# Score passes of the 64-wide heads and the compressed branch's matmuls, all over 128 rows

## The chip, the core and the metric

The program runs on one core of a Trainium2 chip. The metric is the device time of one execution, in microseconds (us). The core has a matrix engine (TensorE, PE in the profile), three engines for elementwise work (VectorE or DVE, ScalarE or ACT, GpSimd or POOL) and SyncE (SP), whose queue issues most of the transfers. TensorE multiplies a stationary operand, loaded beforehand by a weight load (PEld), with a moving one that streams through; the stationary operand has as many rows as the contraction is long. Results go to PSUM.

## The reference, cut to what matters

Two residual blocks over 512 tokens of 1024 features, in float32. Block 1 has latent attention (MLA, 96 wide), a sparse attention (NSA, 8 heads of 64 in 2 groups) and a gated MLP; block 2, twice, has 4 differential heads, 12 heads of 64 and a convolved MLP. The parts at issue are the scores of the 64-wide heads, and the compressed branch of NSA, in which 31 compressed keys and values stand for blocks of 32 tokens:

```
s_c = jnp.einsum('bsgrd,bngd->bgrsn', qg, kc) * scale      # 4 heads r of a group g share 31 keys n
p_c = jax.nn.softmax(jnp.where(valid_c, s_c, NEG), axis=-1) * valid_c
o_c = jnp.einsum('bgrsn,bngd->bsgrd', p_c, vc)
...
s_w = jnp.einsum('bcqgrd,bckgd->bcgrqk', qb, kb) * scale   # window; the selected branch and block 2 alike
```

## The kernel before, in words

**Precision.** Every float32 factor is split into a high and a low part of a shorter format (float32r), `hi` by ScalarE and `lo = x - hi` by DVE, and a product is made of `hi*hi`, `hi*lo` and `lo*hi`, which accumulate in one PSUM tile. A head of 64 has half of the array's rows only, so two of the three parts are stacked: `stack_q` puts the queries' high and low part one above the other into a tile of 128 rows (`qa`, by copies on SP), and the keys' high part lies there twice (`ka`). One pass over 128 rows then gives `qh*kh + ql*kh`. The third part, `qh*kl`, is a second pass over 64 rows (`nqh` with `kl` or `qkl` in the rows of the profile).

**Scores.** `scores` (L904) makes a unit of one head and branch: for each of four blocks of 128 queries both passes, 256, 256, 384 and 512 keys wide (256, 256, 384 and 384 in the window), then the softmax with DVE and ScalarE. All matmuls stand at L103 (`mm`), all transposes at L107 (`tr`). `apply_v` transposes the probabilities, splits them and multiplies with the values into `ps_o`.

**Compressed branch.** `cmp_end` makes the compressed keys and values: `kcA` (high part, twice) and `kcL` (low part, twice) with 32 columns for each group, and `vcA`, high and low beside each other, with the same 32 rows four times, for the four heads. `cmp_scores` makes for each head a tile of 32 rows of scores, which ScalarE copies (L1333) into the head's rows of `sT`; and the unit of the window ends with two passes over the 32 rows of its head:

```
mm(ps[:32], kcA[:, g], qa, True, False)
mm(ps[:32], kcL[ro:ro + 64, g], qhi, False, True)
...
mm(po, vcA[rr, g], pch[rr], False, False)
mm(po, vcA[rr, g], pcl[rr], False, True)
```

**Order.** Generators weave the attention units (`pipeline`: the preparation of a unit, the scores of the one before, the values of the one before that) with a filler, the projections and output products whose matmuls write `ps_d` (`merge`). Behind that a scheduler lays out the instructions of each engine before the run, by its own model of their durations, and decides which tile of a pool goes where; each engine then runs its list in order. Tiles of 128x512 come from one pool, `U`, of 67. SP's list holds the loads of weights (L122, L209, into 4 buffers) and the copies of queries (L1299, L1300) and keys (L1278, L1738).

Of the kernel before, what the change touches and what calls it, by code (L numbers as in the profile page):

```python
# [9 lines left out]
F32R = mybir.dt.float32r  # L10
# [9 lines left out]
NB = S // 128  # L20
# [54 lines left out]
def blocks_kernel(ctx: ExitStack, tc: tile.TileContext, A, out):  # L75
# [72 lines left out]
    def fm_weights(src, nk, c0, ncols, r0=0):  # L148
        """Yields (m, [(kt, hi, lo)]) for each tile of 128 columns."""
        for c in range(c0, c0 + ncols, 256):  # L150
            n = min(256, c0 + ncols - c)
            step = 1024 // n
            tiles = [[] for _ in range(n // 128)]
            for k0 in range(0, nk, step):
                k = min(step, nk - k0)
                hi, lo = split(raw_load(src, r0 + 128 * k0, k, c, n))
                for i in range(k):
                    for q in range(n // 128):
                        cs = slice(128 * q, 128 * q + 128)
                        tiles[q].append((k0 + i, hi[:, i, cs], lo[:, i, cs]))  # L160
            for q in range(n // 128):
                yield (c - c0) // 128 + q, tiles[q]

    def fm_start(parts, nk, X):
        """the first two tiles of features of one or two products, k by k; parts: (src, c0, r0, evac)"""
# [18 lines left out]
    def fm_product(src, nk, c0, ncols, X, evac, r0=0, m0=0):  # L184
        """features m0.. of a product whose columns begin at c0"""
# [12 lines left out]
    def tm_product(src, nk, cols, X, evac):  # L198
        """token-major product for the column ranges cols; evac(blk, ps)."""
# [39 lines left out]
    def blend(main, other, ratio):  # L239
        """main's steps, with ratio times as much of other in between; other's cost is not counted"""  # L240
# [22 lines left out]
    def merge(main, filler, ratio, finish=True):  # L263
        """main, with ratio times as much of filler in between. Either may yield a key that the
        other one has to mark before it goes on."""
# [37 lines left out]
    def split_act(src_ap, shape=(128, 512), scale=None, name="x"):  # L303
        """src (fp32) * scale -> hi (ACT), lo (DVE)."""
# [31 lines left out]
    # x, token-major  # L336
# [7 lines left out]
    # per-feature vectors, as columns  # L344
    col = {}

    def load_vectors(eng, name, rows):
# [4 lines left out]
        for nm, ap, n in rows:  # L352
# [3 lines left out]
            elif isinstance(ap, list):  # L356
                # gains that the rotated part of a head does not take here
# [15 lines left out]
    # masks  # L373
# [20 lines left out]
    def rsqrt_cols(dst, src, n):  # L394
        """dst = (src / n + eps) ** -0.5 on small tiles."""
# [10 lines left out]
    # silu(c)  # L406
# [11 lines left out]
    def ada_sums(ws, pool=False, n=512):  # L418
        """per-partition part of a modulation group; ws: list of the group's 8 weight tiles, which
        receives the sum"""  # L420
# [23 lines left out]
    def ada(g):  # L444
        """columns 512g.. of the modulation"""
# [17 lines left out]
    def adas(groups):  # L463
        """the modulation's column groups; each one's sum over partitions follows later"""
# [10 lines left out]
    # the first product, for six tiles of features at once, by quarters of its rows: each quarter  # L475
    # needs its own columns of the first shift and scale only
# [3 lines left out]
    # (first tile of rows, tiles)  # L480
# [27 lines left out]
    # small loads, for later  # L508
# [92 lines left out]
    def mod1_end(c):  # L601
        """a chunk's features of the first shift and scale"""
# [13 lines left out]
    def mod1_step(q, n):  # L616
        """the next n (all with 0) of a quarter's sums"""
# [8 lines left out]
    def angles():  # L626
        """positions times frequencies, and a quarter turn more, in -pi..pi"""
# [154 lines left out]
    def gain_tables(name, tab, gains, half):  # L782
        """tables for a rotation after the gains; one set for each head"""
# [17 lines left out]
    def rope(eng, v, tab, b, half, n, p=128):  # L801
        """v: [p, n, >=2*half]; rotates the first 2*half of the last dim in place."""
# [16 lines left out]
    # compressed blocks: key n ends at 16 n + 31  # L819
# [8 lines left out]
    # lambda of the differential heads  # L828
# [32 lines left out]
    def vsplit(dst, src, scale=None):  # L861
        """dst [128, n, 128] <- src [128, n, 64]: hi | lo"""
# [31 lines left out]
    def to_fm(src, w, o=0):  # L894
        """src: list of NB token-major [128, >=o+w]; -> psum [w, 512]"""
# [8 lines left out]
    def scores(passes, mask, scale, kind, res, gate=None, tok=None):  # L904
        """res gets (P, r): softmax numerators P[q] [128, n] and (gate over denominators) r [128, 4].
        scale is a power of two, so that the scaled scores are exact; tok: a positive factor of each
        query's scores, and its negative."""
# [53 lines left out]
    def apply_v(P, kind, po, vf, start, stop):  # L961
        """transposes P, splits it and accumulates the product with V in po"""
# [32 lines left out]
    def pipeline(units, WO, LAG):  # L995
        """units: generator functions (prep, first, second, perhaps third), each stage one unit
        behind the one before it"""
# [10 lines left out]
    def weave(*gens):  # L1008
        """alternates the steps of generators, each taking its number of steps"""
# [10 lines left out]
    def o_pair(pair, po, i, res, name):  # L1020
        """sums the two halves of po into rows 64i.. of the pair's tile"""
# [134 lines left out]
    # compressed keys and values  # L1156
    CT = [[], []]

    def cmp_prep(i):
        """keys (0) or values (1) and positions, arranged for the product with w1"""  # L1160
# [28 lines left out]
    def cmp_hidden(i):  # L1189
# [12 lines left out]
        # silu through tanh, times two  # L1202
# [10 lines left out]
    kcA = cp.tile([128, 2, 32], F32R, name="kcA")  # L1213
    kcL = cp.tile([128, 2, 32], F32R, name="kcL")
    vcA = cp.tile([128, 2, 128], F32R, name="vcA")
    V.memset(f32(kcA), 0.0)
    V.memset(f32(kcL), 0.0)

    def cmp_end():
        w2k, w2v = (load_w2(A[n][0]) for n in ("cmp_w2_k", "cmp_w2_v"))  # L1220
# [33 lines left out]
        vsplit(vcA, pvc)  # L1254
# [9 lines left out]
        SC.copy(kcA[:, :, 0:31], pk3)  # L1264
        V.tensor_tensor(kcL[:, :, 0:31], pk3, f32(kcA[:, :, 0:31]), op=OP.subtract)
        yield 1.0

    # keys: [hi; hi] and [lo; lo] for both groups
    def dup_keys(o):
        kh, kl = split_act(to_fm([flat(t) for t in NK], 128, o), scale=vcol(("nsa_ks", "nsa_kw")[o // 128], 0),  # L1270
                           name="nk")
        res = []
        for g in range(2):
            own = slice(64 * g, 64 * g + 64)
            a = U(dt=F32R, name="ka")
            l = U(dt=F32R, name="kl")
            for i in range(2):
                nc.sync.dma_start(out=f32(a[64 * i:64 * i + 64]), in_=f32(kh[own]))  # L1278
                nc.sync.dma_start(out=f32(l[64 * i:64 * i + 64]), in_=f32(kl[own]))
            res.append((a, l))  # L1280
        return res
# [9 lines left out]
    def stack_q(src, o, scale=None):  # L1291
        """two heads of 64: H [128,512] and for each head the stacked parts"""
# [9 lines left out]
        return qh, ql, st  # L1302
# [10 lines left out]
    def nsa_units(g):  # L1313
# [3 lines left out]
        def stacks():  # L1317
            yield from need("nsa")
            for pr in range(2):
                qh, ql, st = stack_q([flat(t) for t in NQ], 256 * g + 128 * pr, vcol("nsa_q", 0))  # L1320
                yield 0.43
                for i in range(2):
                    heads.append((st[i], qh[64 * i:64 * i + 64], 64 * i))

        def cmp_scores():
            # compressed branch, four heads at once
            yield from need("cmp")
            sT = U(name="sT")
            for r_, (qa, qhi, ro) in enumerate(heads):
                ps = PS("s", bufs=3)  # L1330
                mm(ps[:32], kcA[:, g], qa, True, False)
                mm(ps[:32], kcL[ro:ro + 64, g], qhi, False, True)
                SC.copy(sT[32 * r_:32 * r_ + 32], ps[:32])  # L1333
                yield 0.43
            ps = PS("t")
# [28 lines left out]
        def unit(r_, br, hd):  # L1364
# [4 lines left out]
            def first():  # L1369
                rate[0] = RU[4 * g + r_]  # L1370
                qa, qhi, ro = heads[r_]
                ka, kl = (KS_, KW_)[br - 1][g]
                st["P"] = []
                yield from scores([(qa, ka), (qhi, kl[ro:ro + 64])], (maskC, maskW)[br - 1], SC8, kind,
# [3 lines left out]
            def second():  # L1378
# [5 lines left out]
                if br == 2:  # L1384
                    pch, pcl = sm["pc"]
                    rr = slice(32 * r_, 32 * r_ + 32)
                    mm(po, vcA[rr, g], pch[rr], False, False)
                    mm(po, vcA[rr, g], pcl[rr], False, True)
# [13 lines left out]
    # merge gates, y = (1 + tanh(z / 2)) * (o @ w_o)  # L1402
# [27 lines left out]
    # residual, feature-major  # L1430
# [31 lines left out]
    def sq_acc(acc, m, src):  # L1462
        """squares of the features; the last tile's stay apart"""
# [7 lines left out]
    def rstd_tm(acc, r):  # L1471
        """r [128, 4] <- (mean of squares + eps) ** -0.5 of the tokens"""
# [9 lines left out]
    def rstd_fm(acc, res):  # L1482
        """the same over the free dimension, for all partitions; in PSUM"""
# [7 lines left out]
    def beside(main, side, at):  # L1491
        """takes a step of side after each of the steps at of main"""
# [36 lines left out]
    def dilated_mask():  # L1529
# [4 lines left out]
        # multiplicity of a distance in the three dilated patterns, as 8*log(m)  # L1534
# [20 lines left out]
    def alternate(a, b, n):  # L1555
        """n steps of a, n of b, ..."""
# [47 lines left out]
    for l in range(2):  # L1604
# [15 lines left out]
        # quads of heads: (columns of q, k, v), group size, rope table, half, mask, first pair of outputs  # L1620
# [101 lines left out]
        def head_unit(P_, h, pair, mask, o0, tag, ratio):  # L1722
            st = {}
            pr, hh = divmod(h, 2)
            own = slice(64 * hh, 64 * hh + 64)

            def prep():
                yield from need(tag)
                if hh == 0:
# [4 lines left out]
                    kas = []  # L1734
                    for j in range(2):
                        ka = U(dt=F32R, name="ka")
                        for i in range(2):
                            nc.sync.dma_start(out=f32(ka[64 * i:64 * i + 64]), in_=f32(kh[64 * j:64 * j + 64]))  # L1738
                        kas.append(ka)
# [184 lines left out]
```

## Time and profile before

| | |
|---|---|
| Time, median of 3 runs | 2229.66 us (2229.32 to 2234.01) |
| Profiled execution, span | 2226.2 us |
| PE busy | 2157.5 us, 97% |
| DVE busy | 1373.3 us, 62% |
| ACT busy | 977.3 us, 44% |
| POOL busy | 311.1 us, 14% |
| DMA queue of SP | 226.01 MB, 33.8% of 16 engines |

The span goes from the first to the last instruction of one profiled execution; the times of the runs hold what lies around it as well, and the page gives no other time for the profiled execution. The attention of block 1 with its filler ends at about 480 us; block 2's attention takes 978 to about 1205 us in the first layer and 1612 to about 1840 us in the second. In a row, `128*128 128x512` is the stationary operand's rows and columns and then the moving operand's. The end of a matmul is modelled, and matmuls are pipelined, so that two of them overlap in the rows; the distance from start to start is what one takes of the engine.

### The profile page before, as it was taken

To read this page: it belongs to the slowest core of one execution; us is meant where nothing else is said; L and a number is where in the kernel's file an instruction comes from. 1 tells how busy PE (TensorE), PEld (TensorE's weight loads), DVE (VectorE), ACT (ScalarE), POOL (GpSimd) and SP (SyncE) were. 2 spreads that over 40 slices of the span, in tenths; PEclk is the share of its full clock that TensorE was granted. 3 is DMA by queue.
4 is the path that set the end of the run, shared out by engine and by line. 5 is a ranking of instruction groups with operands and counts; after the bars stand their busy time and mean duration, and the time that the engine had idled before them with its cause. 6 is when DMAs were issued, how large, how long until landed. Compare 5 with 4: busy or idle time off the path is not lost.

```text
span 2226.2 us, 28323 instructions
## 1 busy us (share of the span) xinstructions
PE 2157.5 (97%) x10349; PEld 1760.7 (79%) x10349; DVE 1373.3 (62%) x2557; ACT 977.3 (44%) x1756; POOL 311.1 (14%) x409
## 2 busy tenths in 40 slices
PE   5999899999999999999999999999999999999998
PEld 4878677777788888888877888888878877888887
DVE  6657877658554333536878673665357787754662
ACT  4456554452322232335655442343356655432441
POOL 4332400003100000111101110011111102100111
PEclk9999999999999999999999999999999999999999
DMA  8222443225343232333333233323344322323231
GB/s 258 80 73 67 116 121 101 80 86 206 98 148 107 85 114 90 98 106 87 96 103 87 87 109 97 104 77 103 95 115 110 90 76 85 114 89 110 77 110 60
DMA packets 211491, 229.09 MB, mean 103 GB/s; under 512 B 12590, under 2 KB 182234, under 8 KB 211352
## 3 DMA queue, kind: packets, MB, share of 16 engines
q1 hardware_dynamic: 209592, 226.01, 33.8%
q8 instruction: 82, 1.34, 0.3%
q0 software_dynamic: 640, 0.55, 0.2%
q10 hardware_dynamic: 1120, 0.72, 0.1%
q14 instruction: 57, 0.47, 0.1%
HBM read 202.06 MB, written 2.10 MB: 92 GB/s over the span
## 4 chain that ended last, share of the span: by engine, by line
PE 71%; DVE 2%; ACT 0%; issue 0%; DMA 0%; DVEq 0%; ACTq 0%
PE ps_d L103 62%; PE ps_s L103 4%; PE ps_t L107 3%; PE ps_o L103 2%; PE ps_t L103 0%; DVE wlo L143 0%; DVE X L1779 0%; ACT p L935 0%; DVE hl L312 0%; DVE p L1707 0%; DMA gf<-in_g_final 0%; DVE p L959 0%; ACT qk L1638 0%; DVE p L931 0%; DVE outt L1895 0%
## 5 line engine op out<-in xcount | busy, mean ns | idle before, releaser
L143 DVE TENSOR_TENSOR wlo<-raw,whi 128x1024 fp32r<-128x1024 f32 (+3 forms) x338 | 415.7, 1232 | 199.6 <-ACT whi L142 196.5
L142 ACT CAST whi<-raw 128x1024 fp32r<-128x1024 f32 (+3 forms) x344 | 346.3, 1009 | 423.7 <-PE ps_d L103 335.4
L103 PE MATMUL ps_d<-hh,whi 128*128 128x512 f32 x1168 | 466.3, 399 | 9.5 <-ACT hh L665 5.9
L103 PE MATMUL ps_d<-hl,whi 128*128 128x512 f32 x1168 | 459.6, 393 | 3.7 <-DVE hl L666 3.7
L103 PE MATMUL ps_d<-hh,wlo 128*128 128x512 f32 x1168 | 458.3, 392 | 0.0
L103 PEld LDWEIGHTS ps_d<-hh,whi 128*128 128x128 f32 x1168 | 220.7, 189 | 63.0 <-ACT hh L665 7.2
L103 PEld LDWEIGHTS ps_d<-hl,whi 128*128 128x128 f32 x1168 | 221.3, 189 | 48.1 <-DVE hl L666 5.4
L103 PEld LDWEIGHTS ps_d<-hh,wlo 128*128 128x128 f32 x1168 | 220.8, 189 | 45.7 <-issue 0.2
L103 PE MATMUL ps_d<-whi,hh 128*128 128x512 f32 (+3 forms) x608 | 219.6, 361 | 1.7 <-DVE v L869 1.0
L103 PE MATMUL ps_d<-whi,hl 128*128 128x512 f32 (+3 forms) x608 | 210.9, 347 | 0.0
L103 PE MATMUL ps_d<-wlo,hh 128*128 128x512 f32 (+3 forms) x608 | 210.1, 346 | 0.0
L103 PE MATMUL ps_d<-fl,whi 128*128 128x512 f32 x528 | 205.6, 389 | 0.0
L103 PE MATMUL ps_d<-fh,whi 128*128 128x512 f32 x528 | 205.6, 389 | 0.0
L103 PE MATMUL ps_d<-fh,wlo 128*128 128x512 f32 x528 | 205.6, 389 | 0.0
L935 ACT ACTIVATE p<-p,sm 128x384 f32<-128x384 f32 (+3 forms) x256 | 144.5, 566 | 69.9 <-DVE sm L931 59.5
L1835 DVE SCALAR_TENSOR_TENSOR ca<-cu,cvT,ca 128x511 f32<-128x511 f32 (+1 forms) x176 | 132.5, 758 | 32.3 <-ACT ca L1833 30.6
L1469 POOL TENSOR_TENSOR acc<-acc,sq 128x512 f32<-128x512 f32 x36 | 56.8, 1578 | 603.3 <-ACT sq L1467 602.6
L1857 POOL TENSOR_TENSOR ca<-ca 128x512 f32<-128x512 f32 x44 | 61.9, 1407 | 520.8 <-DVE ca L1835 472.9
L103 PEld LDWEIGHTS ps_d<-whi,hh 128*128 128x128 f32 x608 | 115.7, 190 | 16.7 <-issue 4.3
L103 PEld LDWEIGHTS ps_d<-whi,hl 128*128 128x128 f32 x608 | 115.5, 190 | 11.9 <-issue 0.5
L103 PEld LDWEIGHTS ps_d<-wlo,hh 128*128 128x128 f32 x608 | 115.8, 191 | 8.0
L1833 ACT ACTIVATE ca<-cu,cvT 128x512 f32<-128x512 f32 x88 | 71.5, 815 | 108.4 <-DVE cu L1831 107.4
(479 smaller groups left out, 3531.9 us busy)
## 6 DMA issues: line engine op xcount, KB each, us to landing
raw<-in_w_up SPq DMA_DIRECT2D x88, 512.0 KB
raw<-in_w_in SPq DMA_DIRECT2D x60, 512.0 KB
aw<-in_ada_w SPq DMA_DIRECT2D x88, 256.0 KB
raw<-in_w_down SPq DMA_DIRECT2D x32, 512.0 KB
raw<-in_ffn_w_gate SPq DMA_DIRECT2D x22, 512.0 KB
raw<-in_ffn_w_up SPq DMA_DIRECT2D x22, 512.0 KB
raw<-in_w_out SPq DMA_DIRECT2D x16, 512.0 KB
raw<-in_ffn_w_down SPq DMA_DIRECT2D x16, 512.0 KB
```

The costliest lines, as they stand in the source:

```text
L103: PE.matmul(o, lhsT=l, rhs=r, start=start, stop=stop)
L107: PE.transpose(o, i, ident[:n, :n])
L142: a = SC.copy(hi, raw)
L143: b = eng.tensor_tensor(lo, raw, f32(hi), op=OP.subtract)
L935: SC.activation(P[q], P[q], AF.Exp, scale=-1.0 if tok is None else tok[1][:, q:q + 1], bias=mn[:, q:q + 1], accum_out=den[:, q:q + 1])
L1469: G.tensor_tensor(acc[0], acc[0], t, op=OP.add)
L1833: SC.activation(a, u, AF.Identity, scale=cvT[:, l, 2, j:j + 1], bias=cvT[:, l, 3, j:j + 1])
L1835: V.scalar_tensor_tensor(a[:, i:], u[:, :S - i], cvT[:, l, 2 - i, j:j + 1], a[:, i:], op0=OP.mult, op1=OP.add)
L1857: G.tensor_tensor(a, a, SG[m], op=OP.mult)
```

## The change

Second passes of scores take the whole of `qa` instead of the high part of the queries, and the keys' low part is laid out twice (`kl`, by copies, also in block 2, where it was used in place). The pass then adds `ql*kl` as well, a fourth part that was left out before. The compressed keys of a group lie in columns 96 to 126 of a tile of zeros, 224 wide; a window of 128 columns is taken from it so that the head's scores fall into rows 32r to 32r+31, and all four heads accumulate into one PSUM tile, which is copied once. The compressed values of a group lie in four tiles of 128 rows, zero but for the head's 32 rows.

```
+    kcA, vcA = [], []
+    def cmp_tiles():
+        for _ in range(2):
+            kcA.append(U((128, 2, 224), F32R, "kcA"))
+            vcA.append(U((128, 4, 128), F32R, "vcA"))
+        for t in kcA + vcA:
+            G.memset(f32(t), 0.0)
...
-        vsplit(vcA, pvc)
+        for r_ in range(4):
+            rr = slice(32 * r_, 32 * r_ + 32)
+            for g in range(2):
+                vsplit(vcA[g][rr, r_:r_ + 1], pvc[rr, g:g + 1])
...
+        for g in range(2):
+            SC.copy(kcA[g][:, 0, 96:127], pk3[:, g])
+            V.tensor_tensor(kcA[g][:, 1, 96:127], pk3[:, g], f32(kcA[g][:, 0, 96:127]), op=OP.subtract)
...
+    def twice(kh, kl, o):
+        res = []
+        for src, name in ((kh, "ka"), (kl, "kl")):
+            t = U(dt=F32R, name=name)
+            for i in range(2):
+                nc.sync.dma_start(out=f32(t[64 * i:64 * i + 64]), in_=f32(src[o:o + 64]))
+            res.append(t)
+        return res
...
+            ps = PS("s", bufs=3)
+            for r_, qa in enumerate(heads):
+                win = slice(96 - 32 * r_, 224 - 32 * r_)
+                mm(ps, kcA[g][:, 0, win], qa, r_ == 0, False)
+                mm(ps, kcA[g][:, 1, win], qa, False, r_ == 3)
                 yield 0.43
+            SC.copy(sT, ps)
...
-                yield from scores([(qa, ka), (qhi, kl[ro:ro + 64])], (maskC, maskW)[br - 1], SC8, kind,
+                yield from scores([(qa, ka), (qa, kl)], (maskC, maskW)[br - 1], SC8, kind,
...
-                    mm(po, vcA[rr, g], pch[rr], False, False)
-                    mm(po, vcA[rr, g], pcl[rr], False, True)
+                    mm(po, vcA[g][:, r_], pch, False, False)
+                    mm(po, vcA[g][:, r_], pcl, False, True)
...
-                    pair["k"] = (kas, kl)
+                    pair["k"] = [twice(kh, kl, 64 * j) for j in range(2)]
...
-                yield from scores([(stk[hh], kas[hh]), (qh[own], kl[own])], mask, SC8, "full", st["P"])
+                yield from scores([(stk, ka), (stk, kl)], mask, SC8, "full", st["P"])
```

The scheduler's lists change with it. In block 1 they stay as they were but for the operands and a few places around the compressed branch; in block 2 the scores and their filler are laid out anew. Three places follow.

TensorE, block 2, the first score unit of a layer, before (`ka` and `qkl` are the keys' parts, `qa` and `nqh` the queries', `ps_d` the filler):

```order
L103 MATMUL ps_s<-ka,qa 128x256
L103 MATMUL ps_s<-qkl,nqh 128x256
L103 MATMUL ps_s<-ka,qa 128x256
L103 MATMUL ps_s<-qkl,nqh 128x256
L103 MATMUL ps_s<-ka,qa 128x384
L103 MATMUL ps_s<-qkl,nqh 128x384
L103 MATMUL ps_s<-ka,qa 128x512
L103 MATMUL ps_s<-qkl,nqh 128x512
```

The same place now:

```order
L103 MATMUL ps_s<-ka,qa 128x256
L103 MATMUL ps_s<-ka,qa 128x384
L103 MATMUL ps_s<-ka,qa 128x512
L103 MATMUL ps_d<-whi,hl 128x512
L103 MATMUL ps_d<-whi,hh 128x512
L103 MATMUL ps_d<-wlo,hh 128x512
L103 MATMUL ps_d<-whi,hl 128x512
L103 MATMUL ps_s<-kl,qa 128x256
L103 MATMUL ps_s<-ka,qa 128x256
L103 MATMUL ps_s<-kl,qa 128x256
L103 MATMUL ps_s<-kl,qa 128x384
L103 MATMUL ps_s<-kl,qa 128x512
```

The first three `ka` passes now come first, then four matmuls of the filler, then the `kl` passes.

SyncE, block 2, the copies of the first pair of 64-wide heads, before:

```order
L1299 DMA qa<-nqh 64x512
L1300 DMA qa<-nql 64x512
L1299 DMA qa<-nqh 64x512
L1300 DMA qa<-nql 64x512
L1738 DMA ka<-qkh 64x512 x4
L209 DMA raw<-in_w_in 128x2x512
```

The same place now:

```order
L1309 DMA qa<-nqh 64x512
L1310 DMA qa<-nql 64x512
L1309 DMA qa<-nqh 64x512
L1310 DMA qa<-nql 64x512
L1284 DMA ka<-qkh 64x512 x2
L1284 DMA kl<-qkl 64x512 x2
L1284 DMA ka<-qkh 64x512 x2
L1284 DMA kl<-qkl 64x512 x2
L209 DMA raw<-in_w_in 128x2x512
```

Each pair has four more copies of 64x512, ahead of the next load of weights.

TensorE, block 1, where the compressed scores stand between the last transposes and value products of MLA (`p`, `mv`); the list of before with -, of now with +:

```order
+L103 MATMUL ps_s<-qa,kcA 128x512 x2
 L107 MATMUL ps_t<-ident,p 128x128 x4
-L103 MATMUL ps_s<-qa,kcA 32x512
-L103 MATMUL ps_s<-nqh,kcL 32x512
+L103 MATMUL ps_s<-qa,kcA 128x512
 L107 MATMUL ps_t<-ident,p 128x128 x2
-L103 MATMUL ps_s<-qa,kcA 32x512
-L103 MATMUL ps_s<-nqh,kcL 32x512
-L103 MATMUL ps_o<-pth,mv 128x512
+L103 MATMUL ps_s<-qa,kcA 128x512
```

The passes keep their number; the first two now stand ahead of the transposes, and the value product that stood between them has moved forward.

## Rows read from the trace of the kernel before

**Rows 1.** Stretch, length; PE, PEld, DVE, ACT, POOL busy us; clock; DMA share; GB/s.

```profile
310.00:480.00 170.00, 169.57 (x782) 121.89 (x781) 118.86 (x363) 85.21 (x212) 0.00 (x0) 0.99 0.22 66
978.00:1050.00 72.00, 72.00 (x391) 58.07 (x390) 42.63 (x112) 40.16 (x93) 10.61 (x24) 1.00 0.40 109
1050.00:1090.00 40.00, 38.78 (x245) 33.91 (x244) 34.40 (x91) 25.10 (x60) 4.31 (x9) 1.00 0.43 117
1090.00:1205.00 115.00, 115.00 (x611) 90.42 (x609) 91.59 (x233) 65.39 (x156) 9.31 (x20) 1.00 0.30 85
```

**Rows 2.** TensorE in order of time: start us, us, engine, line, operation, output<-inputs.

```profile
306.33 0.39 PE L103 MATMUL ps_o<-ptl,mv 128*128 128x512 f32 x1
306.56 0.40 PE L103 MATMUL ps_s<-qa,kcA 128*32 128x512 f32 x1
306.88 0.42 PE L103 MATMUL ps_s<-nqh,kcL 64*32 64x512 f32 x1
307.23 0.44 PE L103 MATMUL ps_o<-pth,mv 128*128 128x384 f32 x1
307.51 0.33 PE L103 MATMUL ps_o<-ptl,mv 128*128 128x384 f32 x1
307.68 0.40 PE L103 MATMUL ps_s<-qa,kcA 128*32 128x512 f32 x1
...
1130.41 0.28 PE L103 MATMUL ps_d<-whi,hl 128*128 128x256 f32 x1
1130.53 0.28 PE L103 MATMUL ps_d<-whi,hh 128*128 128x256 f32 x1
```

**Rows 3.** TensorE in order of time: one score unit of block 2.

```profile
987.48 0.28 PE L103 MATMUL ps_s<-ka,qa 128*128 128x256 f32 x1
987.69 0.38 PE L103 MATMUL ps_s<-qkl,nqh 64*128 64x256 f32 x1
988.00 0.38 PE L103 MATMUL ps_s<-ka,qa 128*128 128x256 f32 x1
...
989.80 0.50 PE L103 MATMUL ps_s<-qkl,nqh 64*128 64x512 f32 x1
990.23 0.50 PE L103 MATMUL ps_d<-whi,hl 128*128 128x512 f32 x1
990.57 0.28 PE L103 MATMUL ps_s<-ka,qa 128*128 128x256 f32 x1
```

**Rows 4.** TensorE and its weight loads in order of time.

```profile
1121.38 0.18 PEld L103 LDWEIGHTS ps_s<-qkl,nqh 64*128 64x128 f32 x1 [0.24 <-issue]
1121.38 0.49 PE L103 MATMUL ps_s<-qkl,nqh 64*128 64x512 f32 x1
```

**Rows 5.** Groups by form, TensorE: busy us, mean ns, idle before.

```profile
L103 PE MATMUL ps_s<-kl,qh 96*128 96x256 f32 x16 | 4.7, 295 | 0.0
L103 PE MATMUL ps_s<-qkl,nqh 64*128 64x256 f32 x48 | 18.3, 381 | 0.0
```

**Rows 6.** TensorE in order of time: compressed values of a head.

```profile
339.64 0.50 PE L103 MATMUL ps_o<-pch,vcA 32*128 32x512 f32 x1
339.99 0.39 PE L103 MATMUL ps_o<-pcl,vcA 32*128 32x512 f32 x1
340.31 0.38 PE L103 MATMUL ps_s<-ka,qa 128*128 128x256 f32 x1
```

**Rows 7.** SyncE in order of time: key copies of a pair.

```profile
983.50 2.45 SPq L1738 DMA_DIRECT2D ka<-qkh  x4
```

**Rows 8.** Waits of the SyncE queue: us in total, times, longest.

```profile
SPq L122 <- DVE wlo L143: 1178.7, 236, 20.4
```

**Rows 9.** Costliest groups of the page: busy us, mean ns, idle before.

```profile
L142 ACT CAST whi<-raw 128x1024 fp32r<-128x1024 f32 (+3 forms) x344 | 346.3, 1009 | 423.7 <-PE ps_d L103 335.4
```

**Rows 10.** All engines in order of time: two small operations.

```profile
299.84 0.29 DVE L866 TENSOR_TENSOR vcA<-ps_t,vcA 128x128 fp32r<-128x128 f32 x1 [0.28 <-ACT vcA L865]
...
1121.75 0.62 POOL L1663 COPY rdx<-sm 128x512 f32<-128x512 f32 x1
```

More of the change, by code (lines that the diff above doesn't have):

```diff
@@ L1211, in load_w2 @@
         return t
[L1213 to L1217, printed above, removed]
+    kcA, vcA = [], []
[5 more added lines that the diff above has]
+            G.memset(f32(t), 0.0)
     def cmp_end():
+        cmp_tiles()
         w2k, w2v = (load_w2(A[n][0]) for n in ("cmp_w2_k", "cmp_w2_v"))
@@ L1263, in cmp_end @@
         pk3 = pkc[:, :62].rearrange("p (g n) -> p g n", g=2)
-        SC.copy(kcA[:, :, 0:31], pk3)
-        V.tensor_tensor(kcL[:, :, 0:31], pk3, f32(kcA[:, :, 0:31]), op=OP.subtract)
+        for g in range(2):
+            SC.copy(kcA[g][:, 0, 96:127], pk3[:, g])
+            V.tensor_tensor(kcA[g][:, 1, 96:127], pk3[:, g], f32(kcA[g][:, 0, 96:127]), op=OP.subtract)
         yield 1.0
+    def twice(kh, kl, o):
[6 more added lines that the diff above has]
+        return res
     def dup_keys(o):
@@ L1271, in dup_keys @@
                            name="nk")
[L1272 to L1281, printed above, removed]
+        return [twice(kh, kl, 64 * g) for g in range(2)]
     SC8 = 0.125
@@ L1301, in stack_q @@
             st.append(t)
-        return qh, ql, st
+        return st
     units = []
@@ L1319, in stacks @@
             for pr in range(2):
-                qh, ql, st = stack_q([flat(t) for t in NQ], 256 * g + 128 * pr, vcol("nsa_q", 0))
+                heads.extend(stack_q([flat(t) for t in NQ], 256 * g + 128 * pr, vcol("nsa_q", 0)))
                 yield 0.43
-                for i in range(2):
-                    heads.append((st[i], qh[64 * i:64 * i + 64], 64 * i))
         def cmp_scores():
@@ L1328, in cmp_scores @@
             sT = U(name="sT")
[L1329 to L1333, printed above, removed]
+            ps = PS("s", bufs=3)
[3 more added lines that the diff above has]
+                mm(ps, kcA[g][:, 1, win], qa, False, r_ == 3)
                 yield 0.43
+            SC.copy(sT, ps)
             ps = PS("t")
@@ L1370, in first @@
                 rate[0] = RU[4 * g + r_]
-                qa, qhi, ro = heads[r_]
+                qa = heads[r_]
                 ka, kl = (KS_, KW_)[br - 1][g]
                 st["P"] = []
-                yield from scores([(qa, ka), (qhi, kl[ro:ro + 64])], (maskC, maskW)[br - 1], SC8, kind,
+                yield from scores([(qa, ka), (qa, kl)], (maskC, maskW)[br - 1], SC8, kind,
                                   st["P"], gv[:, :, h, br])
@@ L1385, in second @@
                     pch, pcl = sm["pc"]
-                    rr = slice(32 * r_, 32 * r_ + 32)
-                    mm(po, vcA[rr, g], pch[rr], False, False)
-                    mm(po, vcA[rr, g], pcl[rr], False, True)
+                    mm(po, vcA[g][:, r_], pch, False, False)
+                    mm(po, vcA[g][:, r_], pcl, False, True)
                     o_pair(hd["pair"], po, h % 2, ON, "on")
@@ L1724, in head_unit @@
             pr, hh = divmod(h, 2)
-            own = slice(64 * hh, 64 * hh + 64)
             def prep():
@@ L1733, in prep @@
                     yield 0.43
[L1734 to L1739, printed above, removed]
-                    pair["k"] = (kas, kl)
+                    pair["k"] = [twice(kh, kl, 64 * j) for j in range(2)]
             def first():
                 rate[0] = ratio
-                qh, _, stk = pair["q"]
-                kas, kl = pair["k"]
+                stk = pair["q"][hh]
+                ka, kl = pair["k"][hh]
                 st["P"] = []
-                yield from scores([(stk[hh], kas[hh]), (qh[own], kl[own])], mask, SC8, "full", st["P"])
+                yield from scores([(stk, ka), (stk, kl)], mask, SC8, "full", st["P"])
                 normalise(*st["P"][0])
```

## The prediction

> **What bounds the kernel now.** I read the stretches first, one row for each stage. In the stages that hold the changed passes, the compressed and selected attention of block 1 (310 to 480 us) and the 64-wide heads of block 2 (978 to 1050 and 1090 to 1205 us; the second layer repeats both from 1612 us), TensorE (PE) is busy for all but 0.43 us of 357, while VectorE (DVE) stands at 70%, 59% and 80% [rows 1]. So these stages end when PE has run its list, and what PE saves there counts, as long as DVE keeps up.
>
> But busy is not the same as streaming. The view in order of time shows this by the distance from one matmul's start to the next one's. In a plain run that distance is 0.12 us for 256 columns, 0.17 for 384 and 0.23 for 512 (the steps from 1130.41, 307.51 and 306.33) [rows 2]. A whole score unit of block 2 looks different [rows 3]: eight passes, alternately 128 rows (`ka,qa`) and 64 rows (`qkl,nqh`), take from 987.48 to 990.23, 2.75 us, where their widths (four of 256, two of 384, two of 512) need 4 x 0.12 + 2 x 0.17 + 2 x 0.23 = 1.28. The full-height matmul behind them still takes 0.34 instead of 0.23. Each step between 128 and 64 rows costs about 0.1 us on either side, and the engine counts as busy meanwhile. The weight loads say why: the load of the 64-row pass starts at 1121.38, in the same 10 ns as its matmul and after 0.24 us of idle that no other engine ended [rows 4]; it isn't loaded beside the matmul before. It is the number of rows and not the second pass as such: MLA's second passes over 96 rows last 295 ns on average at 256 columns, those over 64 rows 381 [rows 5].
>
> **The change part by part.**
>
> *Score passes.* All 160 second passes go from 64 to 128 rows; nothing is added on PE, since a pass takes its columns, and 128-row passes of the same widths keep the plain distance [rows 2]. Per unit that takes away 2.75 - 1.28 + 0.34 - 0.23 = 1.58 us. Units: 8 heads x 2 branches in block 1, and 12 heads x 2 layers in block 2, 40 in all. 40 x 1.58 = 63 us. Units whose passes lie apart between other matmuls cost as much, since each 64-row pass then pays for both its own steps. By stage: 16 units, 25 us, in block 1; 4 units, 6 us, in 978 to 1050; 8 units, 13 us, in 1090 to 1205; the last two again in the second layer.
>
> *Compressed scores.* Per head now 128x32 and 64x32: from 306.56 to 307.23 and 0.28 for the 384-wide matmul behind, against 0.23 + 0.23 + 0.17 [rows 2]: 0.32 us, 8 heads, 2.6 us. The new form has the same two passes, over 128 rows and all 128 columns.
>
> *Compressed values.* Two 32-row passes per head: 0.35 and 0.32 instead of 0.23 each [rows 6], and about 0.1 before and behind as above: 0.40 x 8 = 3.2 us. The rows of zeros cost nothing on PE.
>
> The row of 306.33 shows that going from 128x128 to 128x32 costs nothing: 0.23 to the next start [rows 2]. The Trainium skill (TensorEngine Tiling, Key Properties) says that a change of tiling mode, which there includes tiling by columns, drains the engine; by that the step into the 32 columns should cost another 0.1, 8 times, and the sum would be 0.8 us more. The row decides: only the step in rows is counted.
>
> Gross: 63 + 2.6 + 3.2 = 69 us.
>
> *DVE behind a faster PE.* If the stages shrank by this much, 310 to 480 (all the compressed work and 16 units, 31 us) would last 139 us with 118.86 us of DVE, 86%; 1090 to 1205 would last 102 with 91.59, 90%; 978 to 1050, 66 with 42.63, 65% [rows 1]. The nearest row is the stage of differential heads, 1050 to 1090, where DVE stands at 86% and PE is without work for 1.22 us of 40, 3% [rows 1]. I take 3% of 139 and 4% of 102 twice: 4 + 8 = 12 us given back. The ends: nothing, if all of DVE's idle time is slack; and 31 + 2 x 13 = 57 us, if DVE's idle time in these stages (51 and 23 us) doesn't shrink at all because it is the latency of softmax steps that PE waits for in its fixed order.
>
> *Keys through a transfer.* Block 2 gets four more copies of 64x512 per pair of heads, 12 pairs, 48 in all. Four of them occupy SP for 2.45 us [rows 7]. Queued behind them on SP are the weight loads. Those wait for the release of their buffers anyway (SP's wait on the low parts of weights, 1178.7 us in total) [rows 8], and ScalarE's idle before it splits weights is ended mostly by PE (335.4 of 423.7 us) and not by a transfer [rows 9]: I take nothing, and 12 x 2.45 = 29 us is the far end. The waiting instruction on PE is now the `kl` pass, with all of PE's list behind it. In the first pair of a layer the first key copy is issued at 983.50 and its first pass starts at 987.48, 4 us later [rows 3, 7]; `kl` follows two issues (1.2 us) behind, so it may be ready up to 1.2 us later than `ka`. The new order puts two more `ka` passes and four others (0.17 + 5 x 0.23, about 1.3 us) in between, which covers it: nothing taken, 2 x 1.2 = 2.4 us at the far end; later pairs are prepared a whole unit ahead. Below nothing I see no reason for either.
>
> *Compressed branch, small work.* Seven more splits of 32 rows on ScalarE and on DVE, each as long as the nearest row, 0.29 us, at most: 2 us on each, in 280 to 310; one more split of keys. Four clears of 448 or 512 columns on GpSimd, by its copy of 512 columns 0.62 us each, 2.5 us [rows 10], at the start of the last step of the compressed keys. ScalarE copies the scores once per group instead of four times, off the path. I take 1 us lost; the ends are 0 and 4.5. The four tiles now lie in the common pool until block 1's attention ends, and the high parts of the queries are freed earlier in exchange (four tiles when both groups are up): nothing.
>
> Sum: -69 + 12 + 0 + 1 = -56 us on a profiled span of 2226.2, so 2170. The profile gives its own execution as this span only; the timed runs' median is 3.5 us above it (2229.66), for what lies around, and I keep that: 2174 us.
>
> **The rivals.**
>
> (a) Softmax latency takes over: PE reaches the transposes of a unit before DVE has normalised them, and most of the gain in the dense stages turns into waits. For it: 90% of DVE in 1090 to 1205. Against: PE waits for almost nothing there today, and some of DVE's idle 51 and 23 us must be slack [rows 1]. With half of the 57 us lost instead of 12: -69 + 28 + 1, 2190; with all of it, 2219. It decides from about 30 us of waits on.
>
> (b) The 64-row passes don't pay for their height but for something they keep, say the switch of key tile in the same bank, and the change does nothing to them: then only small losses, 2229 to 2233. Against: the 96-row passes, which have the same switch and last 295 ns [rows 5].
>
> (c) The passes lose an overlap. Two halves of the array could work beside each other, and a 128-row pass would take that away. The place is the step from a 64-row pass into its neighbours; the price, if each of the 160 passes had been half hidden, is half a pass, 0.08 us on average (80 passes of 256 columns, 48 of 384, 32 of 512): 13 us on top, and no gain, 2243. The Trainium skill (TensorE: Matmul & The Clock Gate, Part 3: Packing small matmuls) has the rule: passes of few rows at different row positions run concurrently, so that padding them to 128 gives speed away. Here it decides only if any 64-row pass starts early, and none does: the distance around it grows, to 0.31 at 256 columns [rows 3], which speaks against this case.
>
> (d) PE gains more than I take, because DVE costs it nothing: 2226.2 - 68 + 3.5, 2162.
>
> **How the numbers follow.** My forecast, 2165 to 2190 with 2174 as the value: 0.72. (d), 2157 to 2165: 0.12. (a) beyond 2190: 0.11. (b): 0.03. (c) or a larger loss through the new transfers: 0.02. About 4.5 us, 0.2%, is what a measurement here can tell from no change. All cases but (b) and (c) are faster: 0.95, with 0.03 for the same and 0.02 for slower. For 8 in 10 I take 2158 to 2193.
>
> **What would show it.** Right: starts of `kl,qa` passes 0.12, 0.17 or 0.23 us behind the `ka` pass, loads of weights lying beside the matmul before, PE's share about as high as now over a shorter span, DVE's share up to 84 to 90% in the dense stages, with 10 to 15 us of new waits of PE on DVE or ScalarE. Wrong: the distance around `kl,qa` stays at 0.31 (b), or PE's idle before transposes and value products adds up to more than 30 us (a), or PE waits at the first `kl` pass of pairs for its copy.

## The result and the profile after

The changed kernel takes 2180.29 us (median of 4 runs, 2176.72 to 2182.13) against 2231.34 for the kernel before: a ratio of 0.9773, 95% interval [0.976, 0.9786], 51 us faster. The prediction said 2174, with 2158 to 2193 for 8 in 10.

The profiled spans are 2226.2 and 2180.2, 46 us apart. Of the 5 us between that and the timed gain, 3.2 lie between the first matmul and the first MLA score, where TensorE (PE) has the same list in both: 136.65 us in the trace of before, 139.82 in the trace of after, with a granted clock of 0.91 and 0.86 between 60 and 100 us of the latter. Over all profiles below this stretch comes out at 136 to 140 us, whatever the kernel, so I leave it out of the comparison.

The stages follow from the starts of the same matmuls in both traces, in us. A quad is four heads of block 2: A the differential ones, B, C and D the 64-wide ones; the last row is called the tail below.

| stage | before | changed | difference | gross gain predicted |
|---|---|---|---|---|
| first compressed score to block 1's output product | 182.5 | 153.5 | -29.0 | 31 |
| block 2, quad C, per layer | 55.5 | 49.6 | -5.9, -5.9 | 6 |
| block 2, quad A (unchanged passes) | 57.7 | 57.7 | 0 | 0 |
| block 2, quads B and D (first B to last D score) | 91.5 | 86.3, 85.8 | -5.2, -5.8 | 13 |
| from there to the sums of the next norm | 35.6 | 36.9 | +1.3, +1.2 | 0 |

So the gain is there almost whole in block 1 and in quad C, and some 8.5 us per layer are missing from quads B and D and the tail behind them.

What the change was to do on PE, it did. Two stretches in order of time from the trace of after, which answer to [rows 3] and [rows 6]:

```profile
962.93 0.39 PE L103 MATMUL ps_d<-whi,hl 128*128 128x512 f32 x1
963.15 0.28 PE L103 MATMUL ps_s<-kl,qa 128*128 128x256 f32 x1
963.27 0.28 PE L103 MATMUL ps_s<-ka,qa 128*128 128x256 f32 x1
963.39 0.46 PE L103 MATMUL ps_s<-kl,qa 128*128 128x256 f32 x2
...
337.53 0.40 PE L103 MATMUL ps_o<-pch,vcA 128*128 128x512 f32 x1
337.76 0.40 PE L103 MATMUL ps_o<-pcl,vcA 128*128 128x512 f32 x1
338.00 0.28 PE L103 MATMUL ps_s<-ka,qa 128*128 128x256 f32 x1
```

Here every pass of 256 columns starts 0.12 us behind the one before it, where 0.21 and 0.31 stood; the compressed value passes have 0.23, where 0.35 and 0.32 stood. The weight loads of the same place lie beside the matmul ahead, as [rows 4] showed they did not: the load for 963.15 starts at 962.93, together with the matmul before.

```profile
962.93 0.19 PEld L103 LDWEIGHTS ps_s<-kl,qa 128*128 128x128 f32 x1
963.16 0.19 PEld L103 LDWEIGHTS ps_s<-ka,qa 128*128 128x128 f32 x1
```

The groups by form (busy us, mean ns, idle before) have 282 ns for the second passes of 256 columns, 381 in [rows 5]. The first passes carry something new, 3.8 us of waiting for the key copies:

```profile
L103 PE MATMUL ps_s<-ka,qa 128*128 128x256 f32 x80 | 22.0, 288 | 3.8 <-DMA ka<-qkh 3.8
L103 PE MATMUL ps_s<-kl,qa 128*128 128x256 f32 x80 | 21.3, 282 | 0.0
```

The windows of block 2's first layer after (quad C, quads B and D, the tail; columns as in [rows 1]):

```profile
961.70:1011.30 49.60, 49.60 (x304) 43.40 (x303) 32.94 (x84) 29.68 (x69) 7.61 (x20) 1.00 0.49 131
1069.00:1155.40 86.40, 82.87 (x489) 69.84 (x489) 70.87 (x179) 50.40 (x119) 5.38 (x10) 1.00 0.42 110
1155.40:1192.30 36.90, 34.09 (x159) 26.87 (x158) 31.83 (x50) 22.15 (x40) 10.65 (x6) 1.00 0.28 86
```

In B and D PE now stands idle for 3.5 us of 86.4, and VectorE (DVE) is at 82%, below the 84 to 90% that the prediction expected. The waits of PE from 1062 to 1190 (us in total, times, longest) say on what:

```profile
PE ps_s L103 <- DMA ka<-qkh: 2.1, 2, 1.1
PE ps_d L103 <- ACT ox_h L308: 1.7, 2, 1.0
PE ps_d L103 <- DVE X L1780: 1.4, 2, 0.8
PE ps_s L103 <- DVE wlo L143: 0.7, 1, 0.7
```

Neither transposes behind a normalisation nor value products are in front: it is key copies, and products of `w_out` for which the output parts (`ox_h`) or the residual (`X`) come late. SyncE (SP) in order of time, where one of the waits for `ka` begins; it answers to [rows 7]:

```profile
1087.04 0.53 SPq L122 DMA_DIRECT2D raw<-in_w_out  x1
1088.50 1.82 SPq L1284 DMA_DIRECT2D ka<-qkh  x2
1090.41 1.19 SPq L1284 DMA_DIRECT2D kl<-qkl  x2
1091.66 1.25 SPq L1284 DMA_DIRECT2D ka<-qkh  x2
1093.01 2.83 SPq L1284 DMA_DIRECT2D kl<-qkl  x2
```

And PE at the same place (in brackets what it waited for):

```profile
1095.97 0.35 PE L103 MATMUL ps_s<-ka,qa 128*128 128x256 f32 x1 [1.12 <-DMA ka<-qkh]
```

The copies issued at 1088.50, those of the second pair of heads in B and D, are first read at 1095.97, 7.5 us later and after 1.12 us of waiting. In the trace of before the four copies of the same pair were issued together and first read 6.9 us later, without a wait:

```profile
1120.92 2.39 SPq L1738 DMA_DIRECT2D ka<-qkh  x4
1127.78 0.28 PE L103 MATMUL ps_s<-ka,qa 128*128 128x256 f32 x1
```

So PE did not come sooner behind the issue; the copy came later. The transfers around it differ. The windows of 10.5 us up to that pass, in the trace of after and in that of before:

```profile
1086.00:1096.50 10.50, 9.38 (x75) 9.00 (x75) 7.87 (x23) 5.11 (x14) 3.66 (x6) 1.00 0.93 223
```

```profile
1117.30:1127.80 10.50, 10.50 (x84) 9.94 (x83) 7.51 (x22) 5.23 (x14) 3.66 (x6) 1.00 0.72 192
```

The DMA engines are busy to 93% (223 GB/s) against 72% (192 GB/s). That share alone does not decide: in the second layer of the changed kernel the same pair's copies, issued at 1712.73, are read at 1718.93 without a wait, with 93% in the 10.5 us before.

### The profile page after: what moved, and what is told of

It is laid out like the page before. It is cut to its first block, busy times and chain, and to the rows that moved or that the text cites. A ratio compares the mean times of both kernels' runs of the same rounds, so it can differ in the third digit from the quotient of the medians.

```text
span 2180.2 us, 28513 instructions
## 1 busy us (share of the span) xinstructions
PE 2099.8 (96%) x10349; PEld 1756.3 (81%) x10349; DVE 1371.4 (63%) x2563; ACT 972.1 (45%) x1758; POOL 312.0 (14%) x413
## 4 chain that ended last, share of the span: by engine, by line
PE 82%; DVE 8%; DMA 3%; ACT 3%; issue 3%; POOL 2%; SPq 0%; ACTq 0%; DVEq 0%; POOLq 0%
PE ps_d L103 70%; PE ps_s L103 5%; PE ps_t L107 4%; PE ps_o L103 2%; DMA aw<-in_ada_w 2%; DVE wlo L143 1%; PE ps_t L103 1%; ACT p L935 1%; DMA ka<-qkh 1%; POOL sm L403 1%; DVE acc L430 1%; DVE p L959 1%; DVE ptl L983 1%; DVE p L931 1%; ACT whi L142 0%
```

## The experiments

Two questions were open. First, is it the step between heights that costs, as the prediction says, or something that each 64-row pass has for itself? Second, what takes 8.5 us per layer back in B and D with their tail: DVE behind a faster PE (the prediction's term), or the 48 new key copies (for which it took nothing)?

**The step or the pass.** The kernel before, with the passes of the second query block in turned order, so that two 64-row passes stand next to each other:

```diff
-            for i, (qf, kf) in enumerate(passes):
+            turned = q == 1 and passes[-1][0].shape[0] == 64
+            for i, (qf, kf) in enumerate(passes[::-1] if turned else passes):
```

> The kernel before, with the two passes of the second query block in turned order in all 40 units of 64-wide heads: 128, 64, 64, 128, ... rows instead of 128, 64, 128, 64. No pass changes its height; each unit has one step from 128 to 64 rows and one back less. If the step between heights is what costs: 1.58 / 4 = 0.39 us per unit, less whatever a 64-row pass costs behind another: 40 x 0.39 = 15 us faster, 2216. If each 64-row pass pays for its own height (its weight load never hidden), whatever stands next to it: at most the 0.1 us of the following 128-row pass, 40 x 0.1 = 4 us, 2227. If height has nothing to do with it: 2231.

Measured: 2213.4 us, ratio 0.992 [0.9905, 0.9934], 18 us faster by the medians. By stage: block 1 from 182.5 to 175.2 (16 units, 0.45 each), quad C from 55.5 to 53.9 (4 units, 0.40 each), B and D from 91.5 to 88.5 (8 units, 0.37 each). The unit that [rows 3] showed, in order of time:

```profile
980.12 0.28 PE L103 MATMUL ps_s<-ka,qa 128*128 128x256 f32 x1
980.33 0.50 PE L103 MATMUL ps_s<-qkl,nqh 64*128 64x256 f32 x2
980.76 0.56 PE L103 MATMUL ps_s<-ka,qa 128*128 128x256 f32 x2
981.25 0.44 PE L103 MATMUL ps_s<-qkl,nqh 64*128 64x384 f32 x1
...
982.48 0.50 PE L103 MATMUL ps_d<-whi,hl 128*128 128x512 f32 x1
```

It takes 2.36 us instead of 2.75. The two 64-row passes together have 0.43 us up to the next `ka` pass. In the trace their starts are 980.33 and 980.55: 0.22 behind the first, which has a step ahead of it, and 0.21 behind the second, which has one behind it. A single one between two steps had 0.31 [rows 3], the plain distance is 0.12. So a step adds about 0.09 us to the pass ahead of it and 0.10 to the one behind it, and two passes of one height add nothing for each other. The two steps that are gone make 2 x 0.19 = 0.38 us, what the unit lost. This is what the gross sum rests on, and it falsifies rivals (b) and (c), which had the passes or an overlap of them at work.

Not every change of height costs. In the kernel before, a pass over 96 rows between 128-row ones, in quad A:

```profile
1057.92 0.39 PE L103 MATMUL ps_d<-whi,hl 128*128 128x512 f32 x1
1058.15 0.40 PE L103 MATMUL ps_s<-k,q 96*128 96x512 f32 x1
1058.39 0.40 PE L103 MATMUL ps_d<-whi,hh 128*128 128x512 f32 x1
1058.62 0.40 PE L103 MATMUL ps_d<-wlo,hh 128*128 128x512 f32 x1
```

All three distances are the plain 0.23 or 0.24. So "a step between heights" stands in this document for the steps between 128 rows and 64 or 32.

**The compressed branch alone, and the score passes alone.** The first is the kernel before with only the compressed part of the change:

```diff
-                mm(ps[:32], kcA[:, g], qa, True, False)
-                mm(ps[:32], kcL[ro:ro + 64, g], qhi, False, True)
+                mm(ps, kcA[g][:, 0, win], qa, r_ == 0, False)
+                mm(ps, kcA[g][:, 1, win], qa, False, r_ == 3)
...
-                    mm(po, vcA[rr, g], pch[rr], False, False)
+                    mm(po, vcA[g][:, r_], pch, False, False)
...
```

> The kernel before, with only the compressed branch over 128 rows; the score passes keep their 64 rows. My terms: 2.6 us off the compressed scores and 3.2 off the compressed values, 1 us lost on small work: span 2226 - 5 = 2221, time about 2225, ratio 0.998; all of it between the first compressed score and block 1's output product, 182.5 to about 177.5 us, and block 2 unchanged. Rival (the passes of few rows cost nothing there, being covered by other waits): no change, 2230.

Measured: 2228.47 us against 2231.18, ratio 0.9984 [0.9975, 0.9994]: 3.6 us faster by the ratio, 1 to 6 by its interval. Its stage went from 182.49 to 177.88, 4.6 of the 5.8 us. Block 2's stages are as before to 0.2 us, but for quad C of the first layer: 58.5 us instead of 55.5, without a wait and at a granted clock of 0.94 (0.66 from 990 to 1000 us).

The second is the changed kernel with these lines put back:

> The changed kernel, with the compressed branch (scores and values) as before, over 64 and 32 rows. If the terms add up: the changed kernel plus 5 us, 2185, with block 2's stages as in the changed kernel to 0.5 us. Rival (the passes of few rows cost only because they break a row of passes of equal height, so that once the score passes are even the compressed ones cost more or less than counted): more than 8 us or less than 2 us away from the changed kernel.

Measured: 2181.39 us, ratio 0.9774 [0.9758, 0.9791], 1.1 us from the changed kernel, which is less than either run can tell. By the letter this is the rival's number. The stage says otherwise: 157.4 us against 153.5, 3.8 of the expected 5. The 128-row compressed branch has its gain in its own stage in both pairs; elsewhere the changed kernel is longer (the MLA stage by 1.7 us, B and D by 0.4 and 0.5), which I did not follow up.

**The copies without the gain.** In block 2 the second pass goes back to 64 rows, and the 48 copies stay:

```diff
-                yield from scores([(stk, ka), (stk, kl)], mask, SC8, "full", st["P"])
+                yield from scores([(stk[hh], ka), (qh[own], kl[own])], mask, SC8, "full", st["P"])
```

> The changed kernel, but in block 2 the second score pass goes back to 64 rows (own half of queries and of the doubled low part of keys), with all 48 extra copies made: the price of the copies without PE's gain. If copies cost nothing by themselves: block 2's stages as in the kernel before (quad C 55.5 us, B and D 91.5 us, tail 35.6, in each layer), block 1 as in the changed kernel, so 2231 - 30 = 2200. If the copies delay SP's weight loads or the first passes of pairs whatever PE's pace: 4 us or more per layer above that, 2208 or more.

Measured: 2207.63 us, ratio 0.9893 [0.9876, 0.9909]. Quad C 54.6, B and D 93.3, tail 37.3 in each layer: 3.4 us more than before in the last two, 2.5 with quad C, between the two expectations. The copies, or the order laid around them, cost something even at PE's old pace. The waits of PE in its tail (1170 to 1207):

```profile
PE ps_d L103 <- DVE X L1781: 1.4, 2, 0.8
PE ps_s L103 <- DVE wlo L143: 0.7, 1, 0.7
PE ps_d L103 <- ACT ox_h L308: 0.7, 1, 0.7
```

The tail of the changed kernel (1155 to 1192) has the same three, to 0.1 us; the tail of the kernel before has none of them. So these waits come with the copies, or with that order, and not with the faster PE.

**The gain without the copies.** The same 128 rows in another way: the low keys of both heads stay where they are, and the query of the second pass has zeros in the other head's rows:

```diff
+                    qz = [U(dt=F32R, name="qz") for _ in range(2)]
+                    for j in range(2):
+                        SC.activation(qz[j], f32(qh), AF.Copy, scale=hsel[:, j:j + 1])
...
-                    pair["k"] = [twice(kh, kl, 64 * j) for j in range(2)]
+                    pair["k"] = (kas, kl)
...
-                yield from scores([(stk, ka), (stk, kl)], mask, SC8, "full", st["P"])
+                yield from scores([(stk[hh], kas[hh]), (qz[hh], kl)], mask, SC8, "full", st["P"])
```

> The changed kernel, but block 2's second score pass takes the low keys of both heads where they lie, against queries of which ScalarE has put the other head's half to zero (two 128x512 copies with a column of ones and zeros per pair): all 128 rows as in the changed kernel, and only the four key copies per pair of the kernel before instead of eight. The copies-only run lost 3.4 us per layer in the stage of quads B and D and the tail behind it. If the extra copies, by themselves or through the order that is laid around them, are what gave part of the gain back: 2 to 4 us per layer less in these stages (86.3 and 36.9 us now), 2173 to 2177. If VectorE's share (82 to 86%) is what gives it back: these stages as in the changed kernel within 1 us, 2180.

Measured: 2166.29 us, ratio 0.9715 [0.9699, 0.9731], 64 us faster than before and 13 to 14 faster than the changed kernel; 2173 to 2177 was expected. B and D take 81.7 and 82.2 us, the tail 35.1: 6.4 and 5.4 us less per layer. Quad C is 1.8 us shorter too, but without a wait in either kernel; it holds seven matmuls of the filler less. The window of B and D in the first layer, and one whole unit:

```profile
1064.57:1146.25 81.68, 81.54 (x488) 69.50 (x487) 71.35 (x180) 54.37 (x124) 5.32 (x10) 1.00 0.34 97
```

```profile
959.07 0.36 PE L103 MATMUL ps_s<-ka,qa 128*128 128x256 f32 x1
959.27 0.28 PE L103 MATMUL ps_s<-qkl,qz 128*128 128x256 f32 x1
...
960.20 0.40 PE L103 MATMUL ps_s<-qkl,qz 128*128 128x512 f32 x1
960.43 0.40 PE L103 MATMUL ps_d<-whi,hh 128*128 128x512 f32 x1
```

DVE is at 87% (71.35 of 81.68), more than in the changed kernel, and PE is idle for 0.14 us. So DVE at that share does not by itself hold PE up. The unit takes 1.36 us; the prediction had 1.28 for its eight passes.

**The low keys' copies on another queue.** As many copies as in the changed kernel, half of them issued from ScalarE:

```diff
-[twice(kh, kl, 64 * j) for j in range(2)]
+[twice(kh, kl, 64 * j, (nc.sync, SC)) for j in range(2)]
```

> The changed kernel, with the copies of the keys' low part in block 2 issued from ScalarE instead of SyncE: as many copies and bytes, but no weight load queues behind them on SP. If SP's queue is the price of the copies: 2 to 4 us per layer less, as without copies. If it is the transfers themselves or the order: no gain, 2179 to 2183. If VectorE: no change, 2180.

Measured: 2178.95 us, ratio 0.9771 [0.9757, 0.9786], no difference. The tail is repaired (35.7 us), B and D are not (86.1 and 84.8). The waits of PE there, and of ScalarE from 1065 to 1192:

```profile
PE ps_s L103 <- DMA kl<-qkl: 2.1, 1, 2.1
PE ps_d L103 <- ACT ox_h L308: 1.1, 1, 1.1
...
ACT pt L982 <- DMA kl<-qkl: 5.7, 2, 3.8
```

PE waits for a copy as before, now `kl`, and ScalarE, whose list now holds these copies, has 5.7 us of idle time that the profile puts down to them. Keeping the copies off SP's queue mends the tail and does not save the rest of their price.

**Less work for DVE.** The changed kernel without the normalisation of block 2's 64-wide heads, a step that this kernel leaves out of the computation:

```diff
                 yield from scores([(stk, ka), (stk, kl)], mask, SC8, "full", st["P"])
-                normalise(*st["P"][0])
```

> The changed kernel without the step that divides the numerators of block 2's 64-wide heads by their sums (this part of the computation is left out; four VectorE instructions of 392 ns on average per head, 8 heads, 12.5 us in the stage of quads B and D, of the 71 + 32 us that VectorE is busy there). If VectorE's work or the latency of its steps gives back what the prediction missed: B and D with their tail, 123.2 us now, fall by 5 us or more per layer, 2170 or less. If the copies and the order around them: by less than 2 us per layer, 2177 or more.

Measured: 2170.1 us, ratio 0.9728 [0.971, 0.9746]. B and D with the tail fall by 5.6 and 5.0 us. By itself this speaks for DVE, as the expectation had it; but leaving the copies out had given a little more in the same stages (6.4 and 5.4). The last two runs ask whether these are two losses or one.

**Copies that nobody reads.** The no-copies kernel, with the 48 copies made into a tile that is not used:

```diff
+                        kd = U(dt=F32R, name="kd")
+                        for i in range(2):
+                            nc.sync.dma_start(out=f32(kd[64 * i:64 * i + 64]), in_=f32(kl[64 * j:64 * j + 64]))
```

> The no-copies kernel (2166 us; per layer 81.7 to 82.2 us in quads B and D and 35.1 in the tail), to which the 48 copies of the keys' low part are given back, with nobody reading them: the queue and the transfers have them, and PE waits for none of them. If SP's queue and the transfers are the price (they delay the key copies that PE does read, and the weight loads): B and D and the tail back to 85 or more and 36 or more, 2174 to 2182. If it is PE's own dependence on the low keys' copies, or VectorE: as without copies, within 1 us per layer, 2165 to 2168.

Measured: 2181.2 us, ratio 0.9778 [0.9762, 0.9794]: the whole advantage is gone, though PE reads none of these copies. B and D take 86.0 and 84.0 us, the tail 37.4 and 37.3; so the second layer's B and D stay under the 85 expected, and the first layer's had a granted clock of 0.98, the second's 1.00. The window of B and D in the first layer, and the waits of its tail:

```profile
1067.84:1153.84 86.00, 83.99 (x489) 70.97 (x488) 70.64 (x179) 53.72 (x123) 5.32 (x10) 0.98 0.42 111
```

```profile
PE ps_d L103 <- DVE X L1793: 1.4, 2, 0.8
PE ps_d L103 <- ACT ox_h L308: 1.1, 1, 1.1
PE ps_s L103 <- DVE wlo L143: 0.7, 1, 0.7
```

**Both relieved.** The no-copies kernel, without the normalisation as well:

> The no-copies kernel without the step that divides the numerators of block 2's 64-wide heads by their sums (left out of the computation). Leaving that step out of the changed kernel gave 5.6 us in the first layer and 5.0 in the second for B and D and the tail, leaving the extra copies out gave 6.4 and 5.4. If VectorE and the copies are two prices that add up: another 5 us per layer off, 2156. If they are one and the same loss (a pass that finds its operand late, which either remedy moves out of the way): under 2 us per layer, and not below the 114.5 us that PE's list needs (91.5 + 35.6 less 12.6), 2162 to 2166.

Measured: 2166.38 us, ratio 0.9706 [0.9692, 0.9721], the no-copies kernel to 0.1 us by the medians. B and D take 80.9 and 80.8 us, about 1 us less, the tail the same. Once the copies are gone, 12.5 us less work for DVE in B and D buys next to nothing in the whole time. So it is one loss, and it takes both to have it: with the copies there, the normalisation cost 10 us, and without them nothing; with the normalisation there, the copies cost 13 to 15 us, and without it 4 to 5 (2170.1 against 2166.38, with intervals that overlap). Either remedy takes most of it away; how DVE's relief does that beside the copies I did not follow, and that order is laid anew too.

## Why the prediction was right, and where it was not

- *The mechanism and the gross sum of 69 us* hold in the main. The turned order shows that steps between heights cost, and what one of four pairs of steps costs, 0.39 us in the unit shown against 1.58 / 4 = 0.39 predicted. The no-copies kernel has 64 of the 69 us. Its B and D gain 9.8 and 9.4 us of 13, and 10.6 and 10.7 with the normalisation left out too; the 2 us per layer that still lack stay open.
- *No price for 128x128 to 128x32* was a 0.8 us question; with the changed kernel all passes have 128 columns, and no run here tells it apart.
- *DVE behind a faster PE, 12 us given back* (4 in block 1, 4 per layer in B and D): mis-sized. In block 1 it was 2 at most (29.0 of 31). In B and D it was about 1 per layer, what the no-copies kernel gains there when 12.5 us of DVE's work go; only beside the copies did that work cost 5 per layer. The prediction scaled PE's idle time in the differential stage, 3% at a DVE share of 86% [rows 1], to the others. But the no-copies kernel runs B and D at 87% with 0.14 us of idle PE. So that idle time is not a function of the share alone.
- *Keys through a transfer, 0 us (up to 29)*: this is the step that failed. The copies, with the order laid around them, cost 13 to 15 us, as the no-copies kernel and the unread copies show from either side. The argument looked at SP's spare time [rows 8, 9] and at the first pair of a layer, and took the later pairs to be safe, since they are prepared a whole unit ahead. But weight loads and key copies are issued in bunches, and up to the second pair of B and D the DMA engines were at 93%; PE waited there for a copy issued 7.5 us earlier. Nor did the prediction's warning sign quite fit: PE waits at the first `ka` pass, for copies that share the queue with the new ones, not at a `kl` pass. These direct waits are the smaller part (3.8 us in all); the products of `w_out` and those behind them wait for `ox_h`, `X` and `wlo`, 7.7 us over both layers. That is the sign "new waits of PE on DVE or ScalarE", at less than the 10 to 15 us named; but unread copies bring the same waits in the tail.
- *The sum, -56,* came out at -51 because errors offset each other: 13 us were taken off for DVE and small work where the no-copies kernel lacks 5 of the 69, and nothing for copies that cost 13 to 15. That the time came out within 7 us is, in this part, luck: the forecast was right in time and in the gain, and wrong in its account of the loss. The 3.5 us added to the span were also too many: the changed kernel's profiled execution took 2181.91 us, with a span of 2180.2.
- *Rival (a)* is falsified by its own sign: PE's waits on normalised numerators from 1062 to 1190 are 0.2 us, and 0.9 on weight loads. *Rival (d)*, 2162, is 4 us below what the no-copies kernel reaches, and for the changed kernel it is false.
- *The compressed small work, 1 us*: the stage keeps 3.8 to 4.6 of 5.8 us; the sign and size of its 5 us net hold in the stage, less so in the whole time.

What stays open: how the copies do their harm. Each of these edits changes SP's list, and then every engine's order is laid anew, so the cost of the transfers and that of a less lucky order were not separated. For the transfers speak the DMA share of 0.93 and the copy that came only 7.5 us after its issue; against them, that the second layer had the same share at the same place and no wait; for the order, that copies-only has the tail's waits at PE's old pace, and that moving the copies to another queue mends the tail.

## What to carry to other kernels

Look for steps between 128 rows and 64 or 32 in the distances from start to start, not in the busy share, and price each pair of steps rather than each low pass; putting low passes next to each other recovers a part without any new data. When rows are filled up, fill them with zeros made where the operand is read from (one 0.7 us copy on an engine with spare time) rather than with a second copy of the data by transfer: the added rows were free on PE, but 48 copies of 128 KB, even unread and with the order laid around them, cost a fifth of the gain. And a DVE share near 90% is not a bound as such: read who waits for it.

## What the runs showed of the hardware

- A step between 128 and 64 rows adds to both of its neighbours, the higher as the lower: 0.09 us to the pass ahead and 0.10 to the one behind (0.21 and 0.22 us where 0.12 is plain). A `ka` pass behind a 64-row one has the 0.10 too: in the turned order the two `ka` passes from 980.76 have 0.49 us up to 981.25, where 0.12 + 0.17 would be plain and two steps add the rest. A step between 128 and 96 rows adds nothing (0.23 and 0.24 us at 512 columns, from 1057.92 in the kernel before).
- PE at 128 rows ran beside a DVE that was busy for 87% of an 82 us stage, with 0.14 us of idle time.
- A 128 KB copy of keys, issued while the DMA engines moved 223 GB/s, was read 7.5 us after its issue with 1.1 us of waiting; in the kernel before, with 192 GB/s around it, the same pair's copy was there 6.9 us after its issue and nobody waited. In the second layer of the changed kernel 6.2 us were enough with 231 GB/s, so the rate alone does not tell.
